# Hybrid encoder block on one core: the order of loads and VectorE's work through the first group of the down projection

## Chip, cores and metric

One core of one Trainium2 chip. The metric is the device time of one execution in microseconds (us). Lower is better. Data are float32; every matmul is done in three passes over a high and a low half of each operand (type float32r), so that the result keeps nearly full precision.

## The reference, cut

The kernel computes one encoder layer for 1024 positions and 1024 features. The part that matters here is the gated MLP with its depthwise convolution over positions, from `w_up` through `w_down` to the residual:

```python
    hf = rmsnorm(x, norm_ffn_g[i])
    a = dwconv_centred(hf @ w_up[i], ffn_conv_w[i], ffn_conv_b[i])
    g, u = jnp.split(a, 2, axis=-1)
    x = x + (jax.nn.silu(g) * u) @ w_down[i]

    gate = jax.nn.sigmoid(rmsnorm(x, ple_norm_g[i]) @ w_ple_gate[i])
    x = x + gate * (p[i] @ w_ple_proj[i])
```

Ahead of it stand a combined input projection, a short convolution, latent attention with 8 heads and an output projection; behind it the final norm. `D_FF` is 2816, so there are 22 chunks of 128 rows of `silu(g) * u`.

## The kernel before

All activations are held with features on the 128 partitions and the 1024 positions along the free axis, in tiles of 128x1024; a matmul covers 128x512, half of a tile.

**Up projection.** For each of the 22 chunks a unit of seven matmul groups is run on TensorE (PE). ScalarE (ACT) and VectorE (DVE) read the banks, run the convolution (`conv3`: L261 on ACT, then L262 and L263 on DVE), ACT does the silu (L815), DVE the product (L810), and SyncE (SP) stores the chunk to the DRAM tensor `gud` (L811). The last group of each unit is run inside the next unit, that of unit 21 at the very end (`run_last`). The two unscaled results of a unit lie in the pool `tmp`, which has 4 buffers.

**Down projection.** The 22 chunks are taken in seven groups, `GROUPS = [3, 3, 3, 3, 3, 3, 4]`. For a group of n chunks, each chunk y is loaded from `gud` into a buffer of the same pool `tmp` (L886), and `split` makes its high half on ACT (L267) and its low half on DVE (L268); the pool `gp` has 12 such tiles, six chunks. Then the eight output columns d = 0..7 are taken in pairs. For each pair `load_unit` loads 128x768 weights through SP (L120, three buffers `wraw`), casts the high half on ACT (L128) and makes the low half on DVE (L129), two buffers each. For one column PE runs 18 matmuls into two PSUM banks; of eight banks a column takes two. In the first pair the first two chunks of both columns are run ahead of the third. DVE then adds both banks to the residual x1[d] (L904), which was loaded from the DRAM tensor `x2d` through GpSimd's queue (POOL, L891) in group 0. In the last group the sums also feed the gate's operands.

**What sets the order.** PE's instructions keep the order in which the code is written (`manual_schedule`). Those of the other engines, SP's and POOL's queues too, are placed by a scheduler when the program is built. The scheduler starts SP's loads of the first down weights while the last units of the up projection still run. Each engine then takes its own instructions in the order that was built, and an instruction that waits holds everything behind it on its engine.

Of the kernel before, what the change touches and what calls it, by code (L numbers as in the profile page):

```python
# [18 lines left out]
NC_ = D // P  # L19
# [3 lines left out]
GROUPS = [3, 3, 3, 3, 3, 3, 4]  # L23
# [10 lines left out]
def tile_block(ctx, tc, xT, pT, wlat, wun, wdn, wuq, wukv, vecs, cst, out):  # L34
    nc = tc.nc
# [24 lines left out]
    def ft(dt=F32, shape=None):  # L60
        return tpool[0].tile(shape or [P, S], dt, name="tmp")
# [12 lines left out]
    def pieces(acc):  # L74
        if isinstance(acc, list):
            return [(acc[i], HALF[i]) for i in range(2)]
        return [(acc, slice(0, S))]
# [37 lines left out]
    def vc(i):  # L115
        return vec[:, i:i + 1]
# [8 lines left out]
    def load_unit(src, n=1024, to=None):  # L125
        raw = load_raw(src, n)
        wh, wl = to or (wp.tile([P, n], FR, name="whi"), wp.tile([P, n], FR, name="wlo"))
        act(out=wh, in_=raw, func=AF.Copy)  # L128
        loeng[0].tensor_tensor(out=wl, in0=raw, in1=f(wh), op=ALU.subtract)  # L129
        return wh, wl  # L130
# [14 lines left out]
    def blocks(acc, w, base, xh, xl, ks, n):  # L145
        for k in ks:
            c = slice((base + k) * P, (base + k) * P + P)
            gemm(acc, w[0][:, c], w[1][:, c], xh[k], xl[k], k == 0, k == n - 1)
# [117 lines left out]
    def split(src, hi, lo, eng=None):  # L266
        nc.scalar.copy(out=hi, in_=src)  # L267
        (eng or nc.gpsimd).tensor_tensor(out=lo, in0=src, in1=f(hi), op=ALU.subtract)  # L268

    def split_gain(x, g, hi, lo):  # L270
        act(out=hi, in_=x, func=AF.Copy, scale=g)
        stt(out=lo, in0=x, scalar=g, in1=f(hi), op0=ALU.mult, op1=ALU.subtract)
# [326 lines left out]
    x1 = [xt.tile([P, S], F32, name="xt") for c in range(NC_)]  # L599
    for d in range(NC_):  # L600
        nc.sync.dma_start(out=x1[d], in_=x1d[d])
    x2d = dram.tile([NC_, P, S], F32, name="x2d")
# [105 lines left out]
    gud = dram.tile([NFF, P, S], F32, name="gud")  # L708
# [125 lines left out]
    def bank():  # L834
        return pb.tile([P, 512], F32, name="bk")
# [34 lines left out]
    x1 = [xp.tile([P, S], F32, name=f"x{c}") for c in range(NC_)]  # L870
    gp, g_done = pool("gp", "right", 12)
    gt = lambda: gp.tile([P, S], FR, name="gu")
    hh, hl, wg = [], [], []

    def gate_unit():
        d = len(wg)
        wg.append(load_unit(wun[U_GATE + d], to=(gt(), gt()) if d < 6 else None))

    col = 0
    c0 = 0  # L880
    for g, n in enumerate(GROUPS):
        last = g == len(GROUPS) - 1
        gu = []
        for k in range(n):
            y = ft()
            nc.sync.dma_start(out=y, in_=gud[c0 + k])  # L886
            gu.append((gt(), gt()))
            split(y, *gu[-1], nc.vector)
        if g == 0:
            for d in range(NC_):  # L890
                nc.gpsimd.dma_start(out=x1[d], in_=x2d[d])  # L891
        gh, gl = [x[0] for x in gu], [x[1] for x in gu]
        for d in range(NC_):
            if d % 2 == 0:
                w = load_unit(wdn[:, col:col + 2 * n * P], 2 * n * P)
                col += 2 * n * P
            if d == 0:
                p01 = [[bank(), bank()] for _ in range(2)]
                for i in range(2):
                    blocks(p01[i], w, i * n, gh, gl, range(2), n)  # L900
            p = p01[d] if d < 2 else [bank(), bank()]
            blocks(p, w, d % 2 * n, gh, gl, range(2 if d < 2 else 0, n), n)
            for q, s in pieces(p):
                tt(out=x1[d][:, s], in0=q, in1=x1[d][:, s], op=ALU.add)  # L904
            if last:
                hh.append(xp.tile([P, S], FR, name=f"hh{d}"))
                hl.append(xp.tile([P, S], FR, name=f"hl{d}"))
                split_gain(x1[d], vc(V_PLE + d), hh[d], hl[d])
                if d in (1, 3, 5):
                    gate_unit()  # L910
        c0 += n


    tl, tl_done = pool("tl", "left")
# [211 lines left out]
```

## Time and profile before

| | |
|---|---|
| median of 3 runs | 1356.63 us (1356.61 to 1358.47) |
| profiled execution, its own time | 1356.78 us |
| its span | 1355.0 us |
| mean granted TensorE clock | 0.989 |
| DMA, whole span | 117.38 MB, mean 87 GB/s |
| down projection begins on PE (first matmul with `gu`) | 998.67 us |

The profile is one execution, taken by the hardware profiler. Times in it count from the span's start. A row of the timeline gives the start, the length, the engine, the line of the kernel, the operation, output and inputs by the program's names, and in brackets the idle time of the engine ahead of it with what ended it. `gu` are the halves of a chunk, `whi` and `wlo` those of the weights, `x` the residual, `bk` a PSUM bank, `tmp` a loaded chunk or an intermediate. A row of windows gives for a stretch of time the busy time of PE, PEld (weight loads of PE), DVE, ACT and POOL, then PE's granted clock, the busy share of the DMA engines and the rate in GB/s. In lists of DMA issues the last figure is the median time in us from issue to landing.

### The profile page before, as it was taken

The numbers are of one execution on the slowest core, as the hardware profiler recorded it, in microseconds if no ns is written. First come the engines' busy times: TensorE is split into PE (matmuls) and PEld (weight loads), VectorE is DVE, ScalarE is ACT, GpSimd is POOL, SyncE is SP. The second block draws the span as 40 slices with busy tenths as digits, with TensorE's granted clock in tenths as the row PEclk, the third lists the DMA queues.
The fourth block names the chain that finished last, engine by engine and source line by source line (L and its number), as shares of the span: only waits on it lengthen the run. The fifth ranks groups of instructions, "written<-read, shape, count | busy, mean of one in ns | idle before, by whom it ended". The sixth has DMA issues, their size and how long they took to land.

```text
span 1355.0 us, 16462 instructions
## 1 busy us (share of the span) xinstructions
PE 1323.1 (98%) x6354; PEld 1087.7 (80%) x6354; DVE 1006.1 (74%) x1336; ACT 597.3 (44%) x839; POOL 261.3 (19%) x222
## 2 busy tenths in 40 slices
PE   9999999999999999879999999999999999999997
PEld 7877788888888887658888888888877888888897
DVE  7478923799999957988887888888665555557786
ACT  5323422788888834543443444344331111125433
POOL 0286452455555510000000000000010000000000
PEclk9999999999999999979999999999999999999998
DMA  6201134200000254203222222222174222121123
GB/s 215 78 31 47 47 133 148 78 1 17 1 17 1 68 212 171 94 16 124 78 78 78 94 78 78 78 94 74 66 292 165 95 94 94 55 78 55 49 83 111
DMA packets 38894, 117.38 MB, mean 87 GB/s; under 512 B 4256, under 2 KB 9632, under 8 KB 38816
## 3 DMA queue, kind: packets, MB, share of 16 engines
q1 hardware_dynamic: 35824, 107.30, 22.7%
q10 hardware_dynamic: 1840, 4.83, 0.9%
q0 software_dynamic: 1152, 4.19, 0.8%
q8 instruction: 50, 0.82, 0.3%
q14 instruction: 28, 0.23, 0.0%
HBM read 88.00 MB, written 28.31 MB: 86 GB/s over the span
## 4 chain that ended last, share of the span: by engine, by line
PE 85%; DVE 9%; issue 2%; POOL 2%; ACT 1%; DMA 0%; POOLq 0%; SPq 0%; ACTq 0%
PE bk L139 56%; PE big L139 9%; PE small L139 4%; PE small L534 4%; PE small L547 2%; PE big L504 2%; PE big L508 2%; PE big L506 2%; PE small L546 2%; DVE tmp L163 1%; DVE xt L726 1%; DVE tmp L263 1%; DVE tmp L262 1%; DVE b L726 1%; DVE rbc L164 1%
## 5 line engine op out<-in xcount | busy, mean ns | idle before, releaser
L139 PE MATMUL bk<-gu,whi 128*128 128x512 f32 x704 | 194.7, 398 | 2.8 <-DVE x L904 2.2
L139 PE MATMUL bk<-b,wm 128*128 128x512 f32 x792 | 192.8, 396 | 1.7 <-DVE b L726 1.4
L139 PEld LDWEIGHTS bk<-b,wm 128*128 128x128 f32 x792 | 148.5, 188 | 38.7 <-DVE b L726 2.5
L139 PEld LDWEIGHTS bk<-gu,whi 128*128 128x128 f32 x704 | 133.0, 189 | 36.0 <-issue 2.6
L904 DVE TENSOR_TENSOR x<-bk,x 128x512 f32<-128x512 f32 x112 | 71.9, 687 | 89.3 <-PE bk L139 88.8
L139 PE MATMUL bk<-xt,wm 128*128 128x512 f32 x528 | 129.3, 399 | 7.6 <-DVE xt L726 5.4
L128 ACT ACTIVATE whi<-wraw 128x1024 fp32r<-128x1024 f32 (+2 forms) x55 | 51.3, 933 | 187.7 <-PE bk L139 135.4
L139 PEld LDWEIGHTS bk<-xt,wm 128*128 128x128 f32 x528 | 100.8, 192 | 32.6 <-DVE xt L726 7.8
L139 PE MATMUL bk<-b,whi 128*128 128x512 f32 x352 | 112.4, 400 | 3.1 <-DVE b L726 3.1
L646 POOL TENSOR_TENSOR wm<-wraw,wm 128x512 fp32r<-128x512 f32 x22 | 28.8, 1311 | 448.9 <-ACT wm L645 448.9
L139 PE MATMUL bk<-gu,wlo 128*128 128x512 f32 x352 | 111.3, 397 | 0.0
L790 DVE TENSOR_TENSOR tmp<-bk,tmp 128x512 f32<-128x512 f32 x110 | 75.6, 687 | 30.6 <-PE bk L139 30.5
L521 POOL TENSOR_SCALAR tmp<-tmp,sm 128x256 f32<-128x256 f32 x64 | 70.2, 1097 | 101.2 <-DVE sm L514 98.5
L261 ACT ACTIVATE tmp<-tmp,vec 128x1024 f32<-128x1024 f32 x44 | 54.5, 1238 | 71.1 <-DVE tmp L790 71.1
L511 DVE TENSOR_REDUCE mx<-big 128x1 f32<-128x1024 f32 x64 | 78.0, 1218 | 10.3 <-PE big L508 9.8
L537 DVE TENSOR_TENSOR ptl<-small,pth 128x512 fp32r<-128x512 f32 x128 | 83.1, 679 | 1.2 <-ACT pth L536 0.9
L139 PEld LDWEIGHTS bk<-b,whi 128*128 128x128 f32 x352 | 66.9, 190 | 20.2 <-DVE b L726 4.2
L262 DVE SCALAR_TENSOR_TENSOR tmp<-tmp,vec 128x1023 f32<-128x1023 f32 x48 | 63.9, 1331 | 21.6 <-ACT tmp L261 19.2
L139 PEld LDWEIGHTS bk<-gu,wlo 128*128 128x128 f32 x352 | 66.4, 189 | 16.0
L536 ACT CAST pth<-small 128x512 fp32r<-128x512 f32 x128 | 69.0, 591 | 19.8 <-PE small L534 17.3
L513 ACT ACTIVATE tmp<-big,mx 128x1024 f32<-128x1024 f32 x64 | 72.1, 1127 | 5.2 <-DVE sm L514 2.6
L139 PE MATMUL big<-hh,whi 128*128 128x512 f32 x224 | 71.0, 397 | 3.3 <-DVE tmp L414 3.1
(291 smaller groups left out, 2793.6 us busy)
## 6 DMA issues: line engine op xcount, KB each, us to landing
wraw<-in_wun_dram SPq DMA_DIRECT2D x73, 512.0 KB, 3.2
gud<-tmp SPq DMA_DIRECT2D x22, 512.0 KB, 2.6
tmp<-gud SPq DMA_DIRECT2D x22, 512.0 KB, 4.3
wraw<-in_wdn_dram SPq DMA_DIRECT2D x24, 384.0 KB, 3.1
tmp<-in_xT_dram SPq DMA_DIRECT2D x15, 512.0 KB, 4.1
x1d<-tmp SPq DMA_DIRECT2D x8, 512.0 KB, 2.8
xt<-x1d SPq DMA_DIRECT2D x8, 512.0 KB, 6.4
x2d<-xt SPq DMA_DIRECT2D x8, 512.0 KB, 2.7
```

Of the source, the lines that this page charges most:

```text
L128: act(out=wh, in_=raw, func=AF.Copy)
L139: mm(p, w, x[:, s], start=a, stop=z, skip_group_check=more)
L261: act(out=t, in_=src, func=AF.Identity, scale=vc(w + 1), bias=vc(bias))
L262: stt(out=t[:, 1:S], in0=src[:, 0:S - 1], scalar=vc(w), in1=t[:, 1:S], op0=ALU.mult, op1=ALU.add)
L511: nc.vector.tensor_reduce(m, p, AX.X, ALU.max, negate=True)
L513: act(out=e, in_=p, func=AF.Exp, bias=m, accum_out=su)
L521: nc.gpsimd.tensor_scalar(out=e[:, w:S], in0=e[:, w:S], scalar1=su, scalar2=None, op0=ALU.mult)
L534: nc.tensor.transpose(t[:, k, :], e[:, (g * 4 + k) * P:(g * 4 + k) * P + P], ident)
L536: nc.scalar.copy(out=pth[:, ks, qs], in_=t)
L537: tt(out=ptl[:, ks, qs], in0=t, in1=f(pth)[:, ks, qs], op=ALU.subtract)
L790: add = lambda o, p, q: tt(out=o, in0=p, in1=q, op=ALU.add)
L904: tt(out=x1[d][:, s], in0=q, in1=x1[d][:, s], op=ALU.add)
```

## The change

The loads of the chunks and their splits become a function `chunk(g)`. From the down projection's start to the end of group 0 the order of DVE and SP is now that of the code as well (`order0`). The loads of x are written ahead of the chunks. The chunks of group 1 are loaded and split inside group 0, one behind the sums of each of d = 2, 4 and 6. Tiles, buffers, matmuls and bytes moved stay the same.

```diff
+    starts = [sum(GROUPS[:g]) for g in range(len(GROUPS))]
+    chunks = [[] for _ in GROUPS]
+
+    def chunk(g):
+        y = ft()
+        nc.sync.dma_start(out=y, in_=gud[starts[g] + len(chunks[g])])
+        chunks[g].append((gt(), gt()))
+        split(y, *chunks[g][-1], nc.vector)
+
+    order0 = ExitStack()
+    order0.enter_context(tc.manual_schedule(engines={mybir.EngineType.DVE, mybir.EngineType.SP}))
+    for d in range(NC_):
+        nc.gpsimd.dma_start(out=x1[d], in_=x2d[d])
     for g, n in enumerate(GROUPS):
         last = g == len(GROUPS) - 1
-        gu = []
-        for k in range(n):
-            y = ft()
-            nc.sync.dma_start(out=y, in_=gud[c0 + k])
-            gu.append((gt(), gt()))
-            split(y, *gu[-1], nc.vector)
-        if g == 0:
-            for d in range(NC_):
-                nc.gpsimd.dma_start(out=x1[d], in_=x2d[d])
+        gu = chunks[g]
+        while len(gu) < n:
+            chunk(g)
...
             for q, s in pieces(p):
                 tt(out=x1[d][:, s], in0=q, in1=x1[d][:, s], op=ALU.add)
+            if g == 0 and d in (2, 4, 6):
+                chunk(1)
...
-        c0 += n
+        if g == 0:
+            order0.close()
```

What this moves is seen in the order of the built program. First SP's queue around the start of group 0, before. The loads of `in_wdn` are the down weights, one for each pair of columns; `tmp<-gud` with L886 are the chunks y0, y1, ... as they come; L811 stores the last chunks of the up projection.

```order
L120 DMA wraw_8186<-in_wdn_dram 128x768
L811 DMA gud_4864<-tmp_7779 128x1024
L120 DMA wraw_8236<-in_wdn_dram 128x768
L120 DMA wraw_8286<-in_wdn_dram 128x768
L811 DMA gud_4864<-tmp_7912 128x1024
L120 DMA wraw_8336<-in_wdn_dram 128x768
L886 DMA tmp_8160<-gud_4864 128x1024
L886 DMA tmp_8166<-gud_4864 128x1024
L811 DMA gud_4864<-tmp_8045 128x1024
L120 DMA wraw_8404<-in_wdn_dram 128x768
L990 DMA pj_9833<-pjd_4863 128x512
```

The same place after the change (the chunk loads are now L885, the loads `pj` L1001):

```order
L885 DMA tmp_8170<-gud_4864 128x1024
L885 DMA tmp_8176<-gud_4864 128x1024
L811 DMA gud_4864<-tmp_8045 128x1024
L1001 DMA pj_9836<-pjd_4863 128x512
L1001 DMA pj_9885<-pjd_4863 128x512
L1001 DMA pj_9890<-pjd_4863 128x512
L1001 DMA pj_9923<-pjd_4863 128x512
L885 DMA tmp_8182<-gud_4864 128x1024
L120 DMA wraw_8188<-in_wdn_dram 128x768
L120 DMA wraw_8238<-in_wdn_dram 128x768
L885 DMA tmp_8266<-gud_4864 128x1024
L120 DMA wraw_8294<-in_wdn_dram 128x768
```

Before, the first four weight loads stand ahead of y0, among the stores of the up projection, or next to them. After, the first one (`wraw_8188`) stands behind y2 (`tmp_8182`), and from there on weights and chunks alternate.

Second, ACT around the first casts of the down projection, before. L267 casts a chunk, L128 weights; L261 and L815 are the last convolution and silu of the up projection, L796 and L800 read its banks.

```order
L128 ACTIVATE whi_8188<-wraw_8186 128x768
L800 COPY tmp_7883<-bk_7885 128x512
L645 CAST wm2_8008<-s23_7999 128x1024
L261 ACTIVATE tmp_7985<-tmp_7883,vec_71 128x1024
L796 COPY tmp_8017<-bk_8018 128x512
L815 ACTIVATE tmp_7985<-tmp_7985 128x1024
L261 ACTIVATE tmp_8045<-tmp_7884,vec_71 128x1024
L128 ACTIVATE whi_8238<-wraw_8236 128x768
L800 COPY tmp_8016<-bk_8018 128x512
L267 CAST gu_8162<-tmp_8160 128x1024
```

The same engine after the change, from the first chunk's cast on:

```order
L267 CAST gu_8172<-tmp_8170 128x1024
L261 ACTIVATE tmp_8118<-tmp_8016,vec_71 128x1024
L267 CAST gu_8178<-tmp_8176 128x1024
L261 ACTIVATE tmp_8136<-tmp_8017,vec_71 128x1024
L267 CAST gu_8184<-tmp_8182 128x1024
L815 ACTIVATE tmp_8118<-tmp_8118 128x1024
L128 ACTIVATE whi_8190<-wraw_8188 128x768
L128 ACTIVATE whi_8240<-wraw_8238 128x768
L267 CAST gu_8268<-tmp_8266 128x1024
L128 ACTIVATE whi_8296<-wraw_8294 128x768
```

The first weights' cast (`whi_8188` before, `whi_8190` after) moved from ahead of the last units' work to behind the cast of the third chunk (`gu_8184`) and the last silu.

Third, DVE through the first columns of group 0, before. L904 adds a bank to the residual, L129 makes the low half of weights, L268 the low half of a chunk.

```order
L268 TENSOR_TENSOR gu_8395<-tmp_8392,gu_8394 128x1024
L129 TENSOR_TENSOR wlo_8289<-wraw_8286,whi_8288 128x768
L268 TENSOR_TENSOR gu_8401<-tmp_8398,gu_8400 128x1024
L129 TENSOR_TENSOR wlo_8339<-wraw_8336,whi_8338 128x768
L904 TENSOR_TENSOR x0_8149<-bk_8192,x0_8149 128x512
L904 TENSOR_TENSOR x0_8149<-bk_8193,x0_8149 128x512
L904 TENSOR_TENSOR x1_8150<-bk_8194,x1_8150 128x512
L904 TENSOR_TENSOR x1_8150<-bk_8195,x1_8150 128x512
L904 TENSOR_TENSOR x2_8151<-bk_8242,x2_8151 128x512
L904 TENSOR_TENSOR x2_8151<-bk_8243,x2_8151 128x512
L904 TENSOR_TENSOR x3_8152<-bk_8264,x3_8152 128x512
```

And after the change, where L912 is the sum:

```order
L129 TENSOR_TENSOR wlo_8191<-wraw_8188,whi_8190 128x768
L810 TENSOR_TENSOR tmp_8136<-tmp_8118,tmp_8136 128x1024
L912 TENSOR_TENSOR x0_8149<-bk_8194,x0_8149 128x512
L912 TENSOR_TENSOR x0_8149<-bk_8195,x0_8149 128x512
L912 TENSOR_TENSOR x1_8150<-bk_8196,x1_8150 128x512
L912 TENSOR_TENSOR x1_8150<-bk_8197,x1_8150 128x512
L129 TENSOR_TENSOR wlo_8241<-wraw_8238,whi_8240 128x768
L912 TENSOR_TENSOR x2_8151<-bk_8244,x2_8151 128x512
L912 TENSOR_TENSOR x2_8151<-bk_8245,x2_8151 128x512
L268 TENSOR_TENSOR gu_8269<-tmp_8266,gu_8268 128x1024
L912 TENSOR_TENSOR x3_8152<-bk_8272,x3_8152 128x512
```

Before, the low halves of the third and fourth pair's weights (`wlo_8289`, `wlo_8339`) and of two chunks of group 1 stand ahead of x0's sums, and the sums follow each other. After, x0's and x1's sums stand ahead of the second pair's weights (`wlo_8241`), and one chunk of group 1 (`gu_8269`) stands between the sums of x2 and x3. The pattern goes on so to d = 7.

More of the change, by code (lines that the diff above doesn't have):

```diff
@@ L879, in tile_block @@
     col = 0
-    c0 = 0
+    starts = [sum(GROUPS[:g]) for g in range(len(GROUPS))]
[9 more added lines that the diff above has]
+        nc.gpsimd.dma_start(out=x1[d], in_=x2d[d])
     for g, n in enumerate(GROUPS):
         last = g == len(GROUPS) - 1
-        gu = []
-        for k in range(n):
-            y = ft()
-            nc.sync.dma_start(out=y, in_=gud[c0 + k])
-            gu.append((gt(), gt()))
-            split(y, *gu[-1], nc.vector)
-        if g == 0:
-            for d in range(NC_):
-                nc.gpsimd.dma_start(out=x1[d], in_=x2d[d])
+        gu = chunks[g]
+        while len(gu) < n:
+            chunk(g)
         gh, gl = [x[0] for x in gu], [x[1] for x in gu]
```

## The prediction

> **What bounds the kernel now.** I read the page first: the span, the busy share of TensorE (PE) and, from the view of who waited for whom, what PE waited for. Then PE's own timeline where the down projection begins, because the change touches nothing else, and at last the timelines of the engines that feed it there.
>
> ```profile
> span 1355.0 us, 16462 instructions
> PE 1323.1 (98%) x6354; PEld 1087.7 (80%) x6354; DVE 1006.1 (74%) x1336; ACT 597.3 (44%) x839; POOL 261.3 (19%) x222
> ...
> PE bk L139 <- DVE x L904: 2.2, 1, 2.2
> ...
> PE bk L139 <- DVE gu L268: 0.6, 1, 0.6
> ```
>
> PE is busy for 98% of the span, so a reordering can only remove PE's idle time or add to it. The two last rows are the whole of PE's idle time in the down projection. Here they are in PE's timeline (start, length, idle before):
>
> ```profile
> 998.67 1.10 PE L139 MATMUL bk<-gu,whi 128*128 128x512 f32 x4
> ...
> 1001.26 0.72 PE L139 MATMUL bk<-gu,whi 128*128 128x512 f32 x2 [0.56 <-DVE gu L268]
> 1001.82 0.63 PE L139 MATMUL bk<-gu,wlo 128*128 128x512 f32 x2
> ...
> 1018.61 2.11 PE L139 MATMUL bk<-gu,whi 128*128 128x512 f32 x4 [2.15 <-DVE x L904]
> 1020.51 1.06 PE L139 MATMUL bk<-gu,wlo 128*128 128x512 f32 x2
> 1021.37 1.66 PE L139 MATMUL bk<-gu,whi 128*128 128x512 f32 x4
> 1022.86 0.63 PE L139 MATMUL bk<-gu,wlo 128*128 128x512 f32 x2
> 1023.33 1.10 PE L139 MATMUL bk<-gu,whi 128*128 128x512 f32 x4
> ...
> 1024.73 1.10 PE L139 MATMUL bk<-gu,whi 128*128 128x512 f32 x4
> ```
>
> At full rate six matmuls take 1024.73 - 1023.33 = 1.40 us, 0.233 each. After the 2.15 us wait ten matmuls take 1022.86 - 1018.61 = 4.25 us instead of 2.33: another 1.92 us go. The windows show why: the eighth figure (the granted clock) is halved behind that wait, and stays full behind a wait of 1.55 us elsewhere.
>
> ```profile
> 1015.80:1019.20 3.40, 1.21 (x5) 0.46 (x3) 2.30 (x4) 0.84 (x1) 0.00 (x0) 1.00 0.96 330
> 1019.20:1022.60 3.40, 3.40 (x8) 2.71 (x9) 3.40 (x6) 0.00 (x0) 0.00 (x0) 0.50 1.02 412
> ...
> 166.42 0.70 PE L139 MATMUL big<-hh,whi 128*128 128x512 f32 x2 [1.55 <-DVE tmp L414]
> ...
> 166.40:169.80 3.40, 3.38 (x15) 2.77 (x16) 1.01 (x1) 1.92 (x2) 2.36 (x2) 1.00 0.00 0
> ```
>
> **What the change removes.** The 0.56 us wait goes with the 0.09 us that its first two matmuls lose (1001.82 - 1001.26 = 0.56 for two, where 0.47 is usual): 0.65 us. The second wait came from VectorE (DVE) splitting the weights of later column pairs ahead of x0's sums, so that all eight banks stayed full. In the new order x0's sums follow directly on the first pair's work; that wait goes with its half rate, 2.15 + 1.92 = 4.07 us. Together **-4.72 us**. What is late next is below.
>
> **What it adds at the start of group 0.** Before, SyncE (SP) issued the first weight loads while the up projection still ran; now they stand behind y2, the third chunk (order rows). SP, then DVE, then ScalarE (ACT), in the profile of before:
>
> ```profile
> 945.11 0.33 SPq L120 DMA_DIRECT2D wraw<-in_wdn_dram  x1
> ...
> 992.62 1.77 SPq L990 DMA_DIRECT2D pj<-pjd  x4
> ...
> 997.97 4.78 SPq L886 DMA_DIRECT2D tmp<-gud  x3
> ...
> 996.73 1.22 DVE L268 TENSOR_TENSOR gu<-tmp,gu 128x1024 fp32r<-128x1024 f32 x1
> ...
> 999.99 1.22 DVE L268 TENSOR_TENSOR gu<-tmp,gu 128x1024 fp32r<-128x1024 f32 x1
> ...
> 1003.51 1.22 DVE L268 TENSOR_TENSOR gu<-tmp,gu 128x1024 fp32r<-128x1024 f32 x1
> ...
> 1004.65 1.28 DVE L263 SCALAR_TENSOR_TENSOR tmp<-tmp,vec 128x1023 f32<-128x1023 f32 x1
> ...
> 1001.90 1.05 ACT L267 CAST gu<-tmp 128x1024 fp32r<-128x1024 f32 x1 [0.55 <-DMA tmp<-gud]
> 1002.85 1.06 ACT L815 ACTIVATE tmp<-tmp 128x1024 f32<-128x1024 f32 x1
> ```
>
> y2 goes out at 997.97 because its buffer is y0's, whose split ends at 996.73 + 1.22 = 997.95; that stands in the same place of DVE's order now. SP issues the next load 0.48 us later (four pj loads in 1.77 us, the last one 0.33 long), so w0, the first weights, leaves at 998.45 and not at 945.11. When does it land?
>
> ```profile
> 997.80 3.89 POOL L891 DMA_DIRECT2D x<-x2d  x7 [33.25 <-PE bk L139]
> ...
> tmp<-gud SPq DMA_DIRECT2D x1, 512.0 KB, 3.6
> ...
> wraw<-in_wdn_dram SPq DMA_DIRECT2D x1, 384.0 KB, 9.1
> ...
> DMA packets 907, 3.32 MB, mean 415 GB/s; under 512 B 96, under 2 KB 96, under 8 KB 907
> ...
> q0 software_dynamic: 454, 1.66, 51.3%
> q1 hardware_dynamic: 453, 1.66, 50.8%
> ```
>
> y2 landed 3.6 us after its issue, at 1001.57. POOL's loads of x (q0) take half of 415 GB/s from SP's queue (q1) between 1006 and 1014; 393 KB at the other half are 1.9 us, so w0 lands at about 1003.5. Its cast follows y2's cast and the silu in ACT's order; the silu ends at 1002.85 + 1.06 = 1003.91, and ACT starts the next 0.10 early (1001.90 + 1.05 against 1002.85): 1003.81, whatever landed sooner. The cast of 128x768 takes 0.85 us (row below), and PE starts 0.05 behind its releaser (1001.26 against 999.99 + 1.22): **1004.71 instead of 998.67, 6.04 us**. The ends: landing sooner gains nothing because of the silu; 9.1 us in flight, the slowest row of such a load, gives 1007.55 and 3.74 us more.
>
> The low half of w0 is split behind the L263 that ends at 1005.93; DVE starts the next 0.09 early (1044.30 + 2.69 against 1046.90, in the last rows of this part), takes 0.95, and PE has it at 1006.84. Four half-rate matmuls last 1020.51 - 1018.61 = 1.90 us, to 1006.61: another **0.23 us**. The half rate after the wait is taken from the one here, **1.92 us**. No row has a wait of 6 us, so its ends are 0 (then 1.20 us instead of 0.23 are spent waiting for the low half) and twice the row, 3.84.
>
> The Trainium skill, in "TensorE: Matmul & The Clock Gate", Part 1, says that the clock halves after an idle window of about 3.4 us and returns after as long a busy one. By that page the 2.15 us wait would have cost no clock, and the sum would be +9.2 us: 6.04 + 0.23 + 1.7 + 3.99 - 0.65 - 2.15. The window at 1019.20 with 0.50 speaks against it; for waits of 1.3 us page and trace agree that none is lost.
>
> **What it adds inside group 0.** Columns d = 0..7 go in pairs, with one weight load for each pair. Now the low half of a pair's weights is split only behind the sums of the pair before it; in the unchanged groups it stands one pair ahead. The price is read where the same instructions stand in group 1:
>
> ```profile
> 1044.30 2.69 DVE L904 TENSOR_TENSOR x<-bk,x 128x512 f32<-128x512 f32 x4 [3.12 <-PE bk L139]
> ...
> 1045.46 0.85 ACT L128 ACTIVATE whi<-wraw 128x768 fp32r<-128x768 f32 x1 [6.61 <-PE bk L139]
> ...
> 1045.73 1.10 PE L139 MATMUL bk<-gu,whi 128*128 128x512 f32 x4
> ...
> 1046.90 0.95 DVE L129 TENSOR_TENSOR wlo<-wraw,whi 128x768 fp32r<-128x768 f32 x1
> ```
>
> The pair begins at 1045.73; its fifth matmul, at 1046.66, is the first with the low half. The split behind the sums ends at 1047.85, PE has it at 1047.90: 1.24 us of waiting, and 0.09 for the first two matmuls as above. It comes at d = 2, 4 and 6: **3 x 1.33 = 3.99 us**. The pair at group 1's start is split before x6's sums, early enough.
>
> The chunks of group 1, split behind the sums of d = 2, 4 and 6, are 1.22 us each on DVE in a pair of 36 x 0.233 = 8.4 us, of which sums and weights take 2.69 + 0.95. They cost nothing; without that cover they would cost 3.7 us. The loads of x keep their place on POOL's queue, which waits for PE until 997.80 either way. Behind SP's late w0 stand w1, y3 and w2, all needed 8 us or more after PE's start. The casts and splits that no longer run between 970 and 992 had filled idle time.
>
> **The sum**: -4.72 + 6.04 + 0.23 + 1.92 + 3.99 = **+7.46 us**. The profiled execution took 1356.78 us, 0.15 over the median of 1356.63, so it would become 1364.24, and the median 1364.1.
>
> **Rivals.**
> - *w0 lands as late as the slowest row.* POOL's eight loads are queued at the same moment, and a weight load issued into them took 9.1 us. For it: exactly that traffic. Against it: w0 is directly behind y2, which needed 3.6. PE starts at 1008.45 and waits no more for the low half: +11.0 us, 1367.6.
> - *The bank wait stays.* x0's sums now also wait for x0's load. That load leaves at 997.80 and would have to be 16 us under way. Then 4.07 us are not gained: 1368.2.
> - *w0 is not late: not slower.* If w0's cast were done when the up projection ends, that is if SP and ACT passed w0 ahead of y2, group 0 would start at once and only the waits at d = 2, 4 and 6 would remain: -4.72 + 3.99, or 1355.9; without those too, 1351.9. It decides at a cast ended by 999.3, 0.65 us after the up projection. For it: the load alone is short. Against it: two chains, each sufficient. SP waits for y0's split (997.95), and ACT's cast stands behind the silu (1003.91).
> - *The half rate does not come from the wait.* If it would have come at 1019 anyway, its 1.92 us are not gained back: +9.4 us, 1366.0. Against it: the full clock on both sides of that one window. The page named above is the reason to think of it.
>
> **How the numbers follow.** The forecast has a chance of 0.74, its own range from 1362.7 (no half rate, 3 x 1.2 us) to 1366.0 (twice the half rate). The late w0 has 0.13, the bank wait 0.04, the half rate of another cause 0.03, the w0 that is not late 0.06. The forecast alone leaves a little more than 2 in 10, so the range reaches over the late w0: 1361.5 to 1368.0, the lower end a little under the bounds for what I may have missed. Differences of 0.2%, 2.7 us, are about what a measurement of this kernel can tell from none. Faster by more: 0.02, the last rival without the inner waits. Within: 0.06, its other form and the low tail of the forecast. Slower: 0.92.
>
> **What would show it.** PE's first down matmul waits some 6 us for ACT's whi L128, and the next windows show a clock of 0.50. The first wdn load stands at about 998.4 on SP. Three waits of PE for DVE wlo L129 of some 1.2 us, 9 to 10 us apart, follow, and none for L912. It is wrong if the wdn loads are issued before 990, if PE's first wait is under 1 us, or if group 0 has waits for a DMA.

## The result and the profile after

| | before | after |
|---|---|---|
| median | 1356.72 us (1356.34 to 1359.19, 6 runs) | 1365.07 us (1364.58 to 1366.44, 6 runs) |
| profiled execution, its span | 1355.0 us | 1362.9 us |
| its down projection begins on PE | 998.67 us | 1005.75 us |
| its group 1 begins on PE | 1037.33 us | 1044.88 us |

The changed kernel is slower: the ratio is 1.0059, with a 95% interval from 1.0046 to 1.0072, or 6.2 to 9.8 us. The profiled execution took 1364.80 us. From the page after, and from the view of who waited for whom in the down projection (total, times, longest):

```profile
span 1362.9 us, 16458 instructions
PE 1322.7 (97%) x6354; PEld 1087.4 (80%) x6354; DVE 1005.6 (74%) x1336; ACT 597.2 (44%) x839; POOL 261.0 (19%) x222
```

```profile
PE bk L139 <- ACT whi L128: 6.8, 1, 6.8
PE bk L139 <- DVE wlo L129: 3.2, 3, 1.1
```

PE works as long as before; it idles longer. Both old waits are gone, and four new ones stand in their place. PE's timeline after, with the first of the three waits for the low half:

```profile
996.07 2.90 PE L139 MATMUL bk<-xt,wm 128*128 128x512 f32 x12
1005.75 2.07 PE L139 MATMUL bk<-gu,whi 128*128 128x512 f32 x4 [6.78 <-ACT whi L128]
1007.62 1.05 PE L139 MATMUL bk<-gu,wlo 128*128 128x512 f32 x2
...
1009.59 0.63 PE L139 MATMUL bk<-gu,wlo 128*128 128x512 f32 x2
...
1015.66 1.10 PE L139 MATMUL bk<-gu,whi 128*128 128x512 f32 x4
1017.83 0.73 PE L139 MATMUL bk<-gu,wlo 128*128 128x512 f32 x2 [1.08 <-DVE wlo L129]
1018.40 1.09 PE L139 MATMUL bk<-gu,whi 128*128 128x512 f32 x4
...
1044.88 1.10 PE L139 MATMUL bk<-gu,whi 128*128 128x512 f32 x4
```

Put beside the same matmuls of before, these starts divide the loss into three parts. The first matmul begins at 1005.75 instead of 998.67: 7.08 us later, of which about 0.15 stood already when y2 was issued (998.12 below, 997.97 before). The eleventh matmul begins 1009.59 - 1005.75 = 3.84 us behind the first, where it was 1001.82 - 998.67 = 3.15: 0.69. From there to the first matmul of group 1 it is 1044.88 - 1009.59 = 35.29 us against 1037.33 - 1001.82 = 35.51: a gain of 0.22. Together 7.08 + 0.69 - 0.22 = 7.55 us at the start of group 1; the spans differ by 7.9.

The feeding engines, SP first, then ACT, then DVE, each from its own timeline:

```profile
998.12 0.32 SPq L885 DMA_DIRECT2D tmp<-gud  x1
998.49 0.91 SPq L120 DMA_DIRECT2D wraw<-in_wdn_dram  x2
```

```profile
1002.70 1.05 ACT L815 ACTIVATE tmp<-tmp 128x1024 f32<-128x1024 f32 x1
1004.86 0.84 ACT L128 ACTIVATE whi<-wraw 128x768 fp32r<-128x768 f32 x1 [1.10 <-DMA wraw<-in_wdn_dram]
```

```profile
1014.22 2.69 DVE L912 TENSOR_TENSOR x<-bk,x 128x512 f32<-128x512 f32 x4 [6.15 <-PE bk L139]
1016.83 0.95 DVE L129 TENSOR_TENSOR wlo<-wraw,whi 128x768 fp32r<-128x768 f32 x1
```

w0 leaves SP directly behind y2, as predicted. ACT has the silu behind it at 1003.75 and then waits 1.10 us for w0, which the prediction had landed by then. DVE does the second pair's low half only behind four sums. The view of DMA issues gives w0's time to landing; the two rows below it are the queues' packets, bytes and share between 1001 and 1005:

```profile
wraw<-in_wdn_dram SPq DMA_DIRECT2D x1, 384.0 KB, 6.3
```

```profile
q0 software_dynamic: 270, 1.00, 61.6%
q1 hardware_dynamic: 217, 0.61, 40.6%
```

The windows of after show the half clock (the figure ahead of the DMA share). It sets in while PE still waits and ends some 3 us into the matmuls:

```profile
1002.00:1005.60 3.60, 0.00 (x0) 0.00 (x0) 3.60 (x4) 2.50 (x3) 0.54 (x1) 0.51 1.01 397
1005.70:1009.10 3.40, 3.35 (x8) 2.67 (x9) 2.38 (x3) 0.84 (x1) 0.00 (x0) 0.53 1.03 420
1009.20:1012.60 3.40, 3.40 (x16) 2.74 (x15) 0.00 (x0) 1.05 (x1) 0.00 (x0) 1.00 1.03 415
```

### The profile page after: what moved, and what is told of

Same layout as the page of the kernel before. It is cut to its first block, busy times and chain, and to the rows that moved or that the text cites. A ratio compares the mean times of both kernels' runs of the same rounds, so it can differ in the third digit from the quotient of the medians.

```text
span 1362.9 us, 16458 instructions
## 1 busy us (share of the span) xinstructions
PE 1322.7 (97%) x6354; PEld 1087.4 (80%) x6354; DVE 1005.6 (74%) x1336; ACT 597.2 (44%) x839; POOL 261.0 (19%) x222
## 4 chain that ended last, share of the span: by engine, by line
PE 84%; DVE 9%; issue 2%; POOL 2%; ACT 1%; DMA 1%; POOLq 0%; SPq 0%; ACTq 0%; DVEq 0%
PE bk L139 56%; PE big L139 9%; PE small L139 4%; PE small L534 4%; PE small L547 2%; PE big L504 2%; PE big L508 2%; PE big L506 2%; PE small L546 2%; DVE tmp L163 1%; DVE xt L726 1%; DVE tmp L263 1%; DVE tmp L262 1%; DVE b L726 1%; DVE rbc L164 0%
## 5 line engine op out<-in xcount | busy, mean ns | idle before, releaser
L912 DVE TENSOR_TENSOR x<-bk,x 128x512 f32<-128x512 f32 x112 | 72.1, 685 | 101.5 <-PE bk L139 100.8
L128 ACT ACTIVATE whi<-wraw 128x1024 fp32r<-128x1024 f32 (+2 forms) x55 | 51.3, 933 | 186.0 <-PE bk L139 131.0
L261 ACT ACTIVATE tmp<-tmp,vec 128x1024 f32<-128x1024 f32 x44 | 54.5, 1238 | 71.5 <-DVE tmp L790 71.5
```

The source lines that it names most:

```text
L261: act(out=t, in_=src, func=AF.Identity, scale=vc(w + 1), bias=vc(bias))
```

## The experiments

The kernel before was run beside each group of four (e1 to e4: 1357.32 us, e5 to e8: 1356.98 us, medians of 23 and 11 runs). All ratios are to it; the changed kernel's is 1.0059 (1.0046 to 1.0072). The profiled executions reach the down projection up to 4.1 us later than that of before, by time lost ahead of 610 us, which no edit touches; so starts in different kernels are compared by differences within one trace.

| kernel | what differs from the changed kernel | median us | ratio, 95% interval |
|---|---|---|---|
| e1_w0_first | w0 ahead of the chunks | 1357.54 | 1.0003 (0.9994 to 1.0012) |
| e2_pair_ahead | each pair's weights one pair earlier | 1361.47 | 1.0028 (1.0018 to 1.0037) |
| e3_both | both | 1354.11 | 0.9974 (0.9965 to 0.9984) |
| e4_dve_only | only DVE's order is fixed | 1365.64 | 1.0057 (1.0045 to 1.0070) |
| e5_sp_only | only SP's order is fixed | 1361.11 | 1.0029 (1.0018 to 1.0039) |
| e6_no_inner_chunks | group 1's chunks left to the scheduler | 1372.06 | 1.0105 (1.0088 to 1.0122) |
| e7_x_on_sp | loads of x through SP, not POOL | 1366.00 | 1.0059 (1.0044 to 1.0074) |
| e8_warm | unused matmuls in the first wait | 1363.97 | 1.0049 (1.0034 to 1.0065) |

### e1: the first weights ahead of the chunks

```diff
+    pairs = [n for n in GROUPS for _ in range(NC_ // 2)]
+    done, ahead = [], []
+
+    def weights():
+        n = pairs[len(done)]
+        c = sum(pairs[:len(done)]) * 2 * P
+        done.append(n)
+        return load_unit(wdn[:, c:c + 2 * n * P], 2 * n * P)
...
+        if g == 0:
+            ahead.append(weights())
         while len(gu) < n:
             chunk(g)
...
-                w = load_unit(wdn[:, col:col + 2 * n * P], 2 * n * P)
-                col += 2 * n * P
+                w = ahead.pop(0) if ahead else weights()
```

> Only the first pair's weights (w0) are loaded and split ahead of the chunks of group 0; the rest is as in the changed kernel. Theory (late w0 causes the 6.8 us wait and the 1.5 us of half rate behind it; the three inner waits are a cause of their own): the first wait shrinks to about the 0.56 us of before, the three waits for wlo of 1.08 us stay, the bank wait stays away: 1365.1 - 8.0 = about 1357, no difference to the kernel before. Rival (the chunks split behind the sums, or the traffic at the start, hold group 0 up): still over 1361.

SP's timeline and the view of waits in e1:

```profile
945.37 0.33 SPq L120 DMA_DIRECT2D wraw<-in_wdn_dram  x1
```

```profile
PE bk L139 <- DVE wlo L129: 3.7, 3, 1.6
PE bk L139 <- DVE gu L268: 0.6, 1, 0.6
```

w0 leaves at 945.37, as it did before the change. The first wait and its half clock are gone, the old wait of 0.6 us for the third chunk is back, and the three waits for the low half stay. The time is that of before within its interval. So the late first weights cost the changed kernel some 0.56% (1.0059 - 1.0003), or 7.6 us.

### e2: each pair's weights split one pair ahead

In group 0 each pair's weights are loaded and split ahead of the sums of the pair before it; the first ones stay behind y2. `weights()` is that of e1.

```diff
             if d % 2 == 0:
-                w = load_unit(wdn[:, col:col + 2 * n * P], 2 * n * P)
-                col += 2 * n * P
+                if g == 0:
+                    if not ahead:
+                        ahead.append(weights())
+                    ahead.append(weights())
+                w = ahead.pop(0) if ahead else weights()
```

> Only the order inside group 0 differs from the changed kernel: each later pair's weights are loaded and split one pair ahead. Theory: the three waits for wlo (1.08 us each, 1.34 with the spacing behind it) go, the first wait stays at 6.8 us: 1365.1 - 4.0 = about 1361. Rival (the three waits only take up time that the sums would cost anyway): they turn into waits for the sums L912 or the chunks, still about 1365.

The whole of PE's waits in the down projection, and two rows of its timeline:

```profile
PE bk L139 <- ACT whi L128: 6.7, 1, 6.7
```

```profile
1005.78 2.07 PE L139 MATMUL bk<-gu,whi 128*128 128x512 f32 x4 [6.71 <-ACT whi L128]
...
1010.10 0.63 PE L139 MATMUL bk<-gu,wlo 128*128 128x512 f32 x2
```

The three waits are gone, so they came from the place of L129 behind the sums. Against the changed kernel the ratio is 0.31% lower, or 4.2 us, for three waits of 1.34 us (worked out below). The first ten matmuls are slower here, 1010.10 - 1005.78 = 4.32 us against 3.84, though the first wait is the same to 0.07 us.

### e3: both

```diff
+        if g == 0:
+            ahead.append(weights())
+            ahead.append(weights())
         while len(gu) < n:
             chunk(g)
...
+                if g == 0 and d > 0:
+                    ahead.append(weights())
+                w = ahead.pop(0) if ahead else weights()
```

> Both edits: the weights of the first two pairs ahead of the chunks, each later pair's one pair ahead; the chunks of group 1 stay behind the sums. Theory: PE waits in the down projection only for the 0.56 us of before or not at all, the bank wait of 2.15 us and its half rate stay away: 1356.7 - 4.1 = about 1352.6, faster than both kernels. Rival (the bank wait comes back as soon as PE starts early): about 1356.7.

In the down projection of e3 PE waits once, for 0.6 us, on the third chunk as before the change. Its first matmuls of group 0 and of group 1:

```profile
1000.33 1.10 PE L139 MATMUL bk<-gu,whi 128*128 128x512 f32 x4
...
1034.75 1.10 PE L139 MATMUL bk<-gu,whi 128*128 128x512 f32 x4
```

This is faster than both kernels, by 0.26% (0.16 to 0.35) against before. Group 0 takes 1034.75 - 1000.33 = 34.42 us, where it took 1037.33 - 998.67 = 38.66 before: 4.24 us less, the bank wait with its half clock and nothing else. The median gains 3.2 of them; the profiled execution had lost 1.66 us ahead of group 0 (1000.33 against 998.67), and whether such losses make up the rest is not shown.

### e4: only DVE's order fixed

```diff
-    order0.enter_context(tc.manual_schedule(engines={mybir.EngineType.DVE, mybir.EngineType.SP}))
+    order0.enter_context(tc.manual_schedule(engines={mybir.EngineType.DVE}))
```

> The code of the changed kernel, but only VectorE's order is fixed; SP's loads are placed by the scheduler, so three weight loads stand ahead of the chunks again. Theory (two chains, each sufficient: w0's low half stands behind the third chunk's split on DVE): PE starts at 998.7, does four matmuls and then waits about 6 us for wlo L129, with the half rate and the three inner waits: 1356.7 - 4.7 + 6.0 + 1.5 + 4.0 = about 1363.5. Rival (SP's queue alone makes the first wait): the first wait goes, about 1357.

SP, DVE and PE in e4 (its execution was 4.1 us late before the down projection began):

```profile
949.24 0.33 SPq L120 DMA_DIRECT2D wraw<-in_wdn_dram  x1
```

```profile
1007.64 1.22 DVE L268 TENSOR_TENSOR gu<-tmp,gu 128x1024 fp32r<-128x1024 f32 x1
1008.78 0.95 DVE L129 TENSOR_TENSOR wlo<-wraw,whi 128x768 fp32r<-128x768 f32 x1
```

```profile
1002.80 1.10 PE L139 MATMUL bk<-gu,whi 128*128 128x512 f32 x4
1009.79 1.22 PE L139 MATMUL bk<-gu,wlo 128*128 128x512 f32 x2 [5.89 <-DVE wlo L129]
```

SP loads w0 early and PE begins with its high half on time. Then it stops for the low half, which stands in DVE's fixed order behind the split of y2. DVE's order alone makes group 0 late, without SP's. The three inner waits follow as in the changed kernel (four waits for wlo in all, 9.1 us). The median is some 2 us over the expected 1363.5. With its 4.1 us taken off, the profiled execution is not: its group 1 begins 1048.33 - 1037.33 - 4.13 = 6.87 us late, and the expectation had added 6.8. Why the median is higher stays open.

### e5: only SP's order fixed

```diff
-    order0.enter_context(tc.manual_schedule(engines={mybir.EngineType.DVE, mybir.EngineType.SP}))
+    order0.enter_context(tc.manual_schedule(engines={mybir.EngineType.SP}))
```

> Only SyncE's order is fixed; VectorE's and ScalarE's work goes where the scheduler puts it, as before the change. Theory of two chains, each sufficient for a late start: w0's load stands behind y2 as in the changed kernel, so PE's first matmul of the down projection waits some 6.5 to 7 us, with the half clock behind it (1.5 us), although VectorE is free; but VectorE splits the low halves of later pairs ahead of the sums again, so the three waits of 1.08 us for wlo at d = 2, 4, 6 are gone. About 1361 us. Rival (the late start needs VectorE's order as well): no first wait, about 1353 to 1356. Second rival (the inner waits come from SyncE's order of w1, w2, w3): the three waits stay, now for a DMA or for wlo, about 1365.

PE's only wait in the down projection of e5, two rows of its timeline, and two of DVE's:

```profile
PE bk L139 <- ACT whi L128: 6.7, 1, 6.7
```

```profile
1006.88 2.07 PE L139 MATMUL bk<-gu,whi 128*128 128x512 f32 x4 [6.73 <-ACT whi L128]
...
1011.31 0.78 PE L139 MATMUL bk<-gu,wlo 128*128 128x512 f32 x2
```

```profile
1022.37 0.95 DVE L129 TENSOR_TENSOR wlo<-wraw,whi 128x768 fp32r<-128x768 f32 x1
1023.24 2.48 DVE L912 TENSOR_TENSOR x<-bk,x 128x512 f32<-128x512 f32 x4
```

SP's order alone makes the first wait, at its full 6.7 us. With e4: each of the two orders is enough for a late start, and undoing one of them leaves the other's. The inner waits are gone, since the scheduler again splits the third pair's weights (1022.37) ahead of x0's sums (1023.24). The bank wait does not come back all the same: PE, 6.7 us late, has not filled its eight banks by then (its fifth column begins at 1025.93). So in the changed kernel the lateness by itself would have removed that wait; e1 and e3, where PE is on time, show that DVE's order removes it too.

### e6: the chunks of group 1 left to the scheduler

```diff
-            if g == 0 and d in (2, 4, 6):
-                chunk(1)
```

> The changed kernel without the splits of group 1's chunks inside group 0; they are left to the scheduler behind group 0. Theory: those splits lie in VectorE's idle time, so the waits of 6.8 us and 3 x 1.08 us stay as they are and the time is that of the changed kernel, 1365, unless the chunks now come too late for group 1, which would show as a wait of PE for gu at its start (up to 3 x 1.2 us more). Rival: the three waits of 1.08 us come from the chunks' splits (1.22 us each) standing between the sums and the next pair's low half: then they go, and the time falls by 4 us to 1361.

DVE and PE in e6:

```profile
1021.79 1.23 DVE L268 TENSOR_TENSOR gu<-tmp,gu 128x1024 fp32r<-128x1024 f32 x1 [1.24 <-ACT gu L267]
1022.93 2.48 DVE L912 TENSOR_TENSOR x<-bk,x 128x512 f32<-128x512 f32 x4
1025.33 0.95 DVE L129 TENSOR_TENSOR wlo<-wraw,whi 128x768 fp32r<-128x768 f32 x1
```

```profile
1026.33 1.22 PE L139 MATMUL bk<-gu,wlo 128*128 128x512 f32 x2 [5.25 <-DVE wlo L129]
...
1038.10 0.73 PE L139 MATMUL bk<-gu,wlo 128*128 128x512 f32 x2 [1.08 <-DVE wlo L129]
```

Neither the theory nor the rival was right about the time: it is 6 us longer than the changed kernel's. Left free, the scheduler put all three splits of group 1 ahead of x0's sums, where DVE waits for the chunks one after the other; the sums, and the second pair's low half behind them, come 4 to 5 us late, PE waits 5.25 us and loses its clock once more (its next four matmuls take 1.7 us). The place inside group 0 that the change gives these splits is worth having. What the run was to tell, it tells at the later pairs: at d = 4 no chunk's split stands near, and the wait is the same 1.08 us. The inner waits do not come from the chunks.

### e7: the loads of x through SP's queue

```diff
-    for d in range(NC_):
-        nc.gpsimd.dma_start(out=x1[d], in_=x2d[d])
...
+            if g == 0:
+                nc.sync.dma_start(out=x1[d], in_=x2d[d])
             p = p01[d] if d < 2 else [bank(), bank()]
```

> The loads of x go through SyncE's queue, one for each column behind that pair's weights, and no longer all at once through GpSimd's. Theory (w0 takes 6.3 us from issue to landing because GpSimd's eight loads take some 60% of the DMA engines): w0 lands within about 3.6 us of its issue, ScalarE's cast is then held by the silu alone, PE starts 1.0 to 1.1 us earlier (a first wait of about 5.7 us in place of 6.78), and the time is about 1364. Rival (w0 is held by y2 ahead of it on its own queue): still some 6 us in flight and a first wait of 6.8 us. Either way the half rate and the three waits for wlo stay.

In e7: w0's time to landing, ACT behind the silu, SP's next issues, and PE:

```profile
wraw<-in_wdn_dram SPq DMA_DIRECT2D x1, 384.0 KB, 3.9
```

```profile
1004.43 1.06 ACT L815 ACTIVATE tmp<-tmp 128x1024 f32<-128x1024 f32 x1
1005.39 0.83 ACT L128 ACTIVATE whi<-wraw 128x768 fp32r<-128x768 f32 x1
```

```profile
1009.89 0.32 SPq L811 DMA_DIRECT2D gud<-tmp  x1
...
1011.51 0.46 SPq L120 DMA_DIRECT2D wraw<-in_wdn_dram  x1
```

```profile
1006.27 2.08 PE L139 MATMUL bk<-gu,whi 128*128 128x512 f32 x4 [5.51 <-ACT whi L128]
1008.79 1.22 PE L139 MATMUL bk<-gu,wlo 128*128 128x512 f32 x2 [0.44 <-DVE wlo L129]
...
1011.30 0.63 PE L139 MATMUL bk<-gu,wlo 128*128 128x512 f32 x2
...
1018.69 1.20 PE L139 MATMUL bk<-gu,whi 128*128 128x512 f32 x4 [1.16 <-ACT whi L128]
```

Without POOL's traffic w0 lands in 3.9 us instead of 6.3, ACT casts it as soon as the silu is done, and PE waits 5.51 us instead of 6.78. The edit changes one thing more: w1 is no longer issued directly behind w0, so the run does not tell how much of the 2.4 us is due to POOL and how much to w1.

The first wait fell as expected, but the time did not. The first ten matmuls take 1011.30 - 1006.27 = 5.03 us, 1.19 more than the 3.84 in the changed kernel: they hold a wait of 0.44 us for the low half, and the half clock, read in windows, lasts to 1011.0, over nearly all of them. That takes back nearly all of the 1.27 us; the median is 1366.0, where about 1364 was expected. Further on, x0's load stands behind the last store of the up projection on SP's queue, which goes out at 1009.89, and the second pair's weights behind x0's load. They come late, and PE waits 1.16 us for their high half, in place of the 1.08 us for their low half in the changed kernel.

### e8: PE kept busy through the first wait

```diff
+            if g == d == 0:
+                k = bank()
+                for _ in range(26):
+                    mm(k, onesr, gh[0][:, 0:512], start=True, stop=True)
             if d == 0:
                 p01 = [[bank(), bank()] for _ in range(2)]
```

> 26 matmuls whose result nothing uses, 512 columns each into a spare bank, are put into PE's first wait (26 x 0.233 = 6.1 us of the 6.8). Theory (the half rate of the first ten matmuls behind the wait comes from PE being idle ahead of it): the granted clock stays at 1.00 behind the first wait, the ten matmuls take 2.33 us instead of 3.84, and the time is 1.5 us less, about 1363.6. Rival (the half clock at that place has another cause): it stays, and the time is 1365 or, if the added matmuls push the first real one back, more.

PE's timeline (L908 are the added matmuls) and a window of e8:

```profile
999.12 6.23 PE L908 MATMUL bk<-gu,onesr 128*128 128x512 f32 x26
1006.13 1.21 PE L139 MATMUL bk<-gu,whi 128*128 128x512 f32 x4 [0.79 <-ACT whi L128]
...
1008.78 0.63 PE L139 MATMUL bk<-gu,wlo 128*128 128x512 f32 x2
```

```profile
1005.70:1009.10 3.40, 2.97 (x12) 2.18 (x13) 2.67 (x3) 1.23 (x2) 0.00 (x0) 1.00 1.03 418
```

The clock stays at 1.00, and the ten matmuls take 1008.78 - 1006.13 = 2.65 us instead of 3.84: 1.19 us back. The weights come no sooner. The other 0.32 us over the usual 2.33 stay at the full clock too. So the half clock came from PE being idle. The medians differ by 1.1 us, in the expected direction, but their intervals overlap; the trace decides here, not the time.

## Why the prediction was right, step by step

The mechanism was as forecast. The sum of +7.46 us stands against 7.40 in the trace at the start of group 1 (7.55 less the 0.15 from before the down projection). That it is so close is luck: measured like this, the terms are 6.93 + 0 + 1.51 + 4.02 - 0.82 - 4.24 = 7.40. The first wait cost 0.89 more than forecast, while the half clock (0.41), the low half (0.23) and the old waits (0.34) came out the other way.

- **The old waits go (-0.65 and -4.07).** Right, each 0.17 too small: the first ten matmuls of before took 3.15 us where 2.33 are usual, 0.82 more. A row's idle time leaves out the 0.16 us by which matmuls that follow each other overlap (0.63 long, where the next starts 0.47 later). Between the eleventh matmul and group 1 the three inner waits (3 x 1.34) and the gain of 0.22 leave 4.24 us for the bank wait and its half clock; e3, which adds none of the new waits, gives the same 4.24. The reason was only half of it: e5 shows that a late PE loses this wait whatever DVE's order is.
- **The first wait (6.04).** Right cause, size too small: the first matmul came 6.93 us later once the 0.15 from before are taken off. Mis-sized is the step "w0 lands at about 1003.5": it took 6.3 us and came at about 1004.8, behind the silu instead of ahead of it. The prediction gave SP's queue half of the DMA's rate from the place where both queues had work; in the four microseconds that counted it had 0.61 of 1.61 MB, 38%, and w0's 0.39 MB were not alone in it, since w1 had gone out directly behind w0 (the row at 998.49 is of both). e7, without POOL's loads and without w1 there, gets 5.51 us instead of 6.78, the wait that the silu alone sets. The prediction counted waits for a DMA in group 0 among the signs of being wrong: PE has none, but ACT's 1.10 us for w0 are one, and show the same slip.

The Trainium skill, in "DMA: Bandwidth & Descriptors", section "Queues, rings and completion order", says that each DMA engine takes a packet from each queue in turn. The profile counts 270 packets of POOL's queue and 217 of SP's, of 3.7 and 2.8 KB on average, so here the split was equal neither in packets nor in bytes. Whether what it counts are the packets of that page, no run here shows.

- **The low half of w0 (0.23).** It cost nothing. PE began later and the first four matmuls ran at half clock, so it was ready.
- **The half clock (1.92).** Right cause, as e8 shows, size too large: ten matmuls took 3.84 us, 1.51 over the usual 2.33, and 0.32 of that stay in e8 at the full clock. The range named for it held.
- **The inner waits (3 x 1.33).** Right in size and place: the row at 1017.83 has 1.08 us idle; with the restart the four matmuls ahead of it begin 1017.83 - 1015.66 = 2.17 us earlier, where 0.93 is usual, so 1.24 us, and 0.10 for its own two (0.57 to 1018.40, where 0.47 is usual). e2 takes them away by the place of L129 alone; e6 excludes the chunks.
- **The chunks of group 1 (nothing).** Right where they stand. e6 shows what that place protects from.
- **The rivals.** w0 as late as the slowest row fell: 6.3 us, not 9.1, where the forecast had 5.05 (998.45 to 1003.5). The bank wait is not there. "Two chains, each sufficient" held in e4 and e5, with one correction: DVE's order delays the low half behind y2's split, not the cast on ACT that the prediction named. The half clock of another cause fell: there is none in e1, where PE waits 1.6 us at most.

## What to carry to other kernels

An order written out by hand takes away not only the bad places of a scheduler's order but also the good ones: look at what it had pulled ahead (here the first weights, 53 us early, and each pair's low half) and write that into the order first. The same fixed order with the weights' calls moved ahead went from 0.59% slower than before to 0.26% faster. And undo an order engine by engine before blaming one: here either of two was enough for the delay.

## What the runs showed of the hardware that was not expected

- The half clock has a span of its own, and what a wait costs depends on where in it the matmuls resume. Three first waits of 6.7 to 6.8 us cost the ten matmuls behind them 1.51 us (after), 1.99 (e2: 4.32 - 2.33) and 2.10 (e5: 1011.31 - 1006.88 - 2.33). Read in windows, the clock is 0.50 for 6.8 us in each, from 1002.05, 1003.15 and 1004.80 on, and the matmuls resume 3.7, 2.6 and 2.1 us into it. Behind the 2.15 us wait of before it was 0.50 for 3.4 us (1019.20 to 1022.60); behind the 1.57 us wait of e1 it stayed at 1.00.
- Beside GpSimd's eight loads, and with another weight load directly behind it, a 384 KB load on SP's queue took 6.3 us; without both it took 3.9 (e7).
